# The depthwise convolution of a conformer module as a product of DFT spectra, with tokens in partitions

## The chip, the cores and the metric

The kernel runs on one core of a Trainium2 chip. The metric is the device time of one execution in microseconds (us). Three runs of the kernel before took 1069.94, 1071.75 and 1069.94 us, so its median is 1069.94 us. Of the core's engines this text names TensorE (PE, with its weight load PEld), VectorE (DVE), ScalarE (ACT), GpSimd (POOL) and SyncE (SP, which issues the DMAs).

## The reference

Two transformer blocks act on 256 tokens of width 1024. The change lies in the conv module that opens the second block:

```python
def causal_dwconv_2(x, w, b):            # w: 31 taps x 1024 channels
    y = lax.conv_general_dilated(x, w[:, None, :], window_strides=(1,),
        padding=[(30, 0)], feature_group_count=1024)
    return y + b

def conformer_conv(h, w_pw1, b_pw1, w_dw, b_dw, ln_g, ln_b, w_pw2, b_pw2):
    u = h @ w_pw1 + b_pw1                # 1024 -> 2048
    a, gate = jnp.split(u, 2, axis=-1)
    u = a * jax.nn.sigmoid(gate)
    u = causal_dwconv_2(u, w_dw, b_dw)   # each channel by itself, over time
    u = jax.nn.silu(layernorm(u, ln_g, ln_b))
    return u @ w_pw2 + b_pw2             # 1024 -> 1024
```

`h` is the RMS norm of the residual; everything is fp32. Ahead of the module stands the first block with its feed-forward part (matrix ff2 last), behind it a gated feed-forward part, an attention layer and another feed-forward part.

## The kernel before, in words

The residual `hT` lies with features in partitions: eight tiles of 128 features by 256 tokens. A value that goes through TensorE is split into two fp32r parts, high and low, and a product is three matmuls (high by high, high by low, low by high). Weights come in chunks of 128 x 1024 fp32 (512 KB), in the order of a plan: SP issues the DMA into one of 5 `raw` buffers (L327), ACT rounds it into `hi` (L335), DVE subtracts into `lo` (L336), 7 buffers each; a `raw` buffer is free again after that. `split` (L423, L424) does the same for an activation. PSUM has eight banks under three tags: 4 `acc`, 2 `up`, 2 `ms`. The order in which an engine runs its instructions is drawn up at compile time from the order of the calls, with later calls moved ahead where a cost model sees an engine idle; at run time each engine keeps that order.

The conv module takes its steps in the order of a handwritten list, `CONV_ORDER`:

- **P** (first pointwise product, w_pw1): eight pairs of a value tile and a gate tile, 48 matmuls of 256 columns each, into an `up` bank.
- **G** (`glu`, L929 to L934): scale by the norm's row, sigmoid on ACT (L389), product, into a tile `upad` with 31 leading zeros.
- The convolution itself is divided between two engines, by tap and channel tile. **D** (`conv_dve`, L948): one DVE instruction of 128x256 for each tap. **S** (`conv_rows`, L953, L957): `upad` goes out to a DRAM buffer `far` and comes back four times as `ur`, so that eight shifted copies of a channel lie in eight partitions. **E** (`conv_pe`): POOL builds a sparse weight `dw` (L966), and TensorE adds the taps up in matmuls with 32 output rows (`pcv`). **A** adds both shares (L975, L977).
- **m**, **d**, **M**: mean, deviation and squares of the layer norm over the partitions, through matmuls with a matrix of ones (`pmu`, `pmd`, `pvar`), and then normalising (L1035, L1036), SiLU (L389) and split on the eight tiles.
- The second pointwise product (`pw`, 192 matmuls of 256 columns) accumulates in the 4 `acc` banks; `residual` (L740) adds it to `hT`, and the feed-forward part follows (`ps_up`).

Between P and this product the layer norm is a barrier: it needs the convolution of all 1024 channels. The row of the norm ahead of the module (`ssa`, `ssb`) is computed in the shadow of the first P steps.

Of the kernel before, what the change touches and what calls it, by code (L numbers as in the profile page):

```python
# [28 lines left out]
CONV_ORDER = "P0 G0 P1 P2 G1 P4 P3 G2 P6 G4 D1 S1 S0 G3 S2 E2 S4 A2 P5 P7 G6 E1 G5 D0 E4 A1 A4 S3 S6 G7 E0 A0 D2 w0 E6 E3 A3 w1 S5 E5 S7 m0 d0 E7 A5 w2 D3 M0 A6 d1 A7 w3 d2 M2 M4 d3 M6 M7"  # L29
FRONT_ORDER = "D0 X2 Z0 Q0 S0 X0 W0 Z1 W1 b0 L0 u2 u4 X1 u1 Q1 u0 Q2 L1 T0 E0 B0 G0 T1 u3 Y0 W4 G1 Y1 y0 b4 W2 W5 Q3 b1 W3 b2 V0 W6 y1 n0 W7 b3 b6 V1 b5 O1 b7 O3 O0 O2 a0 s0 N0 q0 w0 q1 o0 w1 w2 o1 w3 o2 o3"  # L30
NSA_ORDER = "W1 K1 W0 R1 G0 K0 H0 g0 p0 h0 R0 H1 n0 r0 C0 p1 n1 w0 h1 V0 w1 V1 c0 t0 r1 c1 p2 C1 u0 t1 n2 w2 u1 c2 w3 o0 p3 r2 w4 t2 o1 n3 u2 t3 w5 r3 o2 w6 o3 t4 c3 w7 t5 t6 o4 o5 u3 t7 o6 o7"
PW_ORDER = (0, 1, 2, 4, 3, 6, 5, 7)
PW_PE = (8, 5, 0, 4, 7, 8, 6, 8)
# [23 lines left out]
def _plan():  # L57
# [51 lines left out]
    for j in PW_ORDER:  # L109
        both("pw1", "conv_w_pw1_2", 0, j, D)  # L110
# [34 lines left out]
def _dve_taps():  # L145

    return [(j, k) for j in range(8) for k in range(31) if (k + 1) % 8 >= PW_PE[j]]


def _rows4(w):  # L150

    w = np.concatenate([np.zeros_like(w[:1]), w], axis=0).reshape(4, 8, 8, 4, 32)
    return w.transpose(0, 4, 2, 1, 3).reshape(P, 256)
# [12 lines left out]
def _w2(w):  # L166
# [20 lines left out]
    ("b_pw1", 16, lambda I: _col(I["conv_b_pw1_2"], 16)),  # L187
    ("w_dw", 256, lambda I: _rows4(I["conv_w_dw_2"][0])),
    ("w_dv", len(_dve_taps()), lambda I: _taps(I["conv_w_dw_2"][0], 8)[:, [31 * j + k for j, k in _dve_taps()]]),
    ("b_dw", 8, lambda I: _col(I["conv_b_dw_2"], 8)),  # L190
# [18 lines left out]
def _offsets(items):  # L209
    o, out = 0, {}  # L210
    for name, n, *_ in items:
# [8 lines left out]
         ("cos", T), ("sin", T), ("cmpadd", 64), ("cmpmul", 64), ("eye4", 32), ("sbmask", P), ("cmask", P)]  # L220
# [3 lines left out]
def _constants():  # L224
# [18 lines left out]
    c["eye4"] = i % 32 == j[:, :32]  # L243
# [23 lines left out]
def kernel(ctx: ExitStack, tc: tile.TileContext, x: bass.AP, mem: bass.AP, stream: bass.AP,  # L267
# [6 lines left out]
    dpool = ctx.enter_context(tc.tile_pool(name="dpool", bufs=2, space=bass.MemoryType.DRAM))  # L274
# [166 lines left out]
    def rt(r):  # L441

        return r.row() if isinstance(r, Norm) else r
# [477 lines left out]
    yc = apool.tile([P, ND, T], F32, tag="b8", name="yc")  # L921
    NH = 31
    dve_taps = _dve_taps()

    def glu(j, ps):

        rt(rs)
        ag = spool.tile([P, 2, T], F32, tag="t2", name="ag", bufs=NT2)
        dve.tensor_mul(ag, ps, rb(rs))  # L929
        sg = spool.tile([P, T], F32, tag="t1", name="sg", bufs=NT1)  # L930
        fn(sg, ag[:, 1, :], AF.Sigmoid, bias=vec("b_pw1", 8 + j))
        up = spool.tile([P, NH + T], F32, tag="t1", name="upad", bufs=NT1)
        pool.memset(up[:, 0:NH], 0.0)
        dve.scalar_tensor_tensor(up[:, NH:], ag[:, 0, :], vec("b_pw1", j), sg, op0=ALU.add, op1=ALU.mult)  # L934
        return up

    def conv_dve(*js):

        first = {j: max([t for t in dve_taps if t[0] == j], default=None) for j in js}
        for k in range(30, -1, -1):  # L940
            for j in js:
                if (j, k) not in dve_taps:
                    continue
                w, u = vec("w_dv", dve_taps.index((j, k))), ups[j][:, k + 1:k + 1 + T]
                if (j, k) == first[j]:
                    act.activation(yc[:, j, :], u, AF.Identity, scale=w, bias=vec("b_dw", j))
                else:
                    dve.scalar_tensor_tensor(yc[:, j, :], u, w, yc[:, j, :], op0=ALU.mult, op1=ALU.add)  # L948

    def conv_rows(up):  # L950

        far = dpool.tile([P, NH + T], F32, tag="far", name="far")
        nc.sync.dma_start(far, up)  # L953
        r = apool.tile([P, 4, T + 7], F32, tag="c4", name="ur", bufs=NC4)
        for b in range(4):
            f = far[32 * b:32 * b + 32]
            nc.sync.dma_start(r[:, b, :], bass.AP(f.tensor, f.offset, [[8, 4], [NH + T, 32], [1, T + 7]]))  # L957
        return r

    def conv_pe(j):  # L960

        ps = acc_bank([P, T], "pcv")
        n = PW_PE[j]
        d = wpool.tile([P, 8, 4, 32], F32, tag="lo", name="dw", bufs=7)
        src = vec("w_dw", 32 * j, 4 * n).rearrange("p (g b) -> p g b", b=4)
        pool.tensor_mul(d[:, :n], src[:, :, :, None].to_broadcast([P, n, 4, 32]),  # L966
                        con("eye4")[:, None, None, :].to_broadcast([P, n, 4, 32]))
        for g in range(n):
            for b in range(4):
                mm(ps[32 * b:32 * b + 32, :], d[:, g, b, :], uss[j][:, b, g:g + T], g == 0, g == n - 1)  # L970
        return ps

    def conv_sum(j, ps):
        if PW_PE[j] == 8:
            act.activation(yc[:, j, :], ps, AF.Identity, bias=vec("b_dw", j))  # L975
        else:
            dve.tensor_add(yc[:, j, :], ps, yc[:, j, :])  # L977


    ups, uss, pcs, pss, w4, ln = {}, {}, {}, {}, [], {}  # L980

    def conv_mean():
        pmu = ms_bank([P, T], "pmu")
        m = spool.tile([P, T], F32, tag="t1", name="yp", bufs=NT1)
        pool.tensor_add(m, yc[:, 0, :], yc[:, 1, :])
        for i, y in enumerate((m, yc[:, 2, :], yc[:, 3, :])):
            mm(pmu, ones, y, i == 0, i == 2)
# [4 lines left out]
    def deviate(p):  # L992
        s = slice(2 * p, 2 * p + 2)
        dve.tensor_sub(yc[:, s, :], yc[:, s, :], rb(ln["mu"]))
# [450 lines left out]
```

## Time and profile before

| | us |
|---|---|
| Median of three runs | 1069.94 |
| Profiled execution, its own time | 1071.3 |
| Its span, first to last instruction | 1069.5 |
| PE / PEld busy | 1035.4 / 957.5 |
| DVE / ACT / POOL busy | 734.8 / 579.7 / 60.2 |

Times in the rows count from the start of the span. A busy PE isn't a PE at its peak: matmuls are pipelined, one of 256 columns shows as about 0.28 us and the next starts after about 0.12 us. The granted clock (PEclk) is a share of 2.4 GHz; 0.5 of it is the lower level of 1.2 GHz, and a value between is a mean over a stretch.

### The profile page before, as it was taken

Reading aid. Unit: us, or ns where it says so; the run is one execution under the profiler, and the core shown is the slowest. Engines: PE = TensorE matmul, PEld = TensorE weight load, DVE = VectorE, ACT = ScalarE, POOL = GpSimd, SP = SyncE. Lnnn points to the kernel's source line nnn. Section 1 sums busy time; section 2 is a strip of 40 time slices with the busy share of each in tenths; the row PEclk is TensorE's granted clock in tenths of the full one; section 3 lists DMA queues with packets and bytes.
Section 4 is the critical chain, followed back from the end, with each engine's and each line's share of the span. In section 5 each row is a group of like instructions: output and inputs, shape, how many; then the busy total and the mean of one; then the engine's idle time right before and its main releaser. Section 6 shows DMA issues by size and latency. Waiting matters only on the chain.

```text
span 1069.5 us, 20182 instructions
## 1 busy us (share of the span) xinstructions
PE 1035.4 (97%) x8113; PEld 957.5 (90%) x8113; DVE 734.8 (69%) x1163; ACT 579.7 (54%) x968; POOL 60.2 (6%) x148
## 2 busy tenths in 40 slices
PE   7999999999999999778999999999999999999998
PEld 6998898999999999537999999998786799999997
DVE  5976568745545587955876677766887468667673
ACT  5766657644444473215654555553867656555551
POOL 0000000000000000320000000000124300000000
PEclk9999999999999999879999999999999999999999
DMA  8753234355655655352555555644742045656641
GB/s 307 241 182 119 79 119 157 131 186 176 195 182 173 195 168 155 96 165 76 186 187 179 181 189 167 197 156 139 226 139 60 2 126 190 199 177 196 182 154 40
DMA packets 52813, 170.43 MB, mean 159 GB/s; under 512 B 5744, under 2 KB 13168, under 8 KB 52720
## 3 DMA queue, kind: packets, MB, share of 16 engines
q1 hardware_dynamic: 51952, 168.09, 48.8%
q8 instruction: 64, 1.05, 0.4%
q0 software_dynamic: 768, 1.05, 0.4%
q14 instruction: 29, 0.24, 0.1%
HBM read 165.99 MB, written 2.08 MB: 157 GB/s over the span
## 4 chain that ended last, share of the span: by engine, by line
PE 87%; DMA 6%; DVE 5%; ACT 1%; issue 1%; SPq 0%; DVEq 0%; ACTq 0%
PE ps_up L288 23%; PE ff L288 9%; PE ps_ff L288 8%; PE ob L288 6%; PE dn L288 6%; PE ps_v L288 3%; PE nl L288 2%; PE pw L288 2%; PE ps_qk L288 2%; PE no L288 2%; PE wo L288 2%; DMA far<-upad 2%; PE npo L288 2%; DVE yc L948 2%; PE ps_nq L288 2%; DMA ur<-far 2%
## 5 line engine op out<-in xcount | busy, mean ns | idle before, releaser
L336 DVE TENSOR_TENSOR lo<-raw,hi 128x1024 fp32r<-128x1024 f32 x296 | 358.2, 1223 | 169.1 <-ACT hi L335 157.3
L335 ACT ACTIVATE hi<-raw 128x1024 fp32r<-128x1024 f32 x296 | 305.2, 1049 | 261.6 <-PE ps_up L288 62.9
L288 PE MATMUL ps_up<-xh,hi 128*128 128x256 f32 x704 | 199.6, 284 | 0.3 <-DVE fv L1057 0.3
L288 PE MATMUL ps_up<-xl,hi 128*128 128x256 f32 x704 | 199.5, 283 | 0.0
L288 PE MATMUL ps_up<-xh,lo 128*128 128x256 f32 x704 | 199.2, 283 | 0.0
L288 PEld LDWEIGHTS ps_up<-xh,hi 128*128 128x128 f32 x704 | 135.1, 192 | 0.9 <-DVE fv L1057 0.5
L288 PEld LDWEIGHTS ps_up<-xl,hi 128*128 128x128 f32 x704 | 135.1, 192 | 0.4
L288 PEld LDWEIGHTS ps_up<-xh,lo 128*128 128x128 f32 x704 | 135.1, 192 | 0.0
L288 PE MATMUL ff<-us,hi 128*128 128x256 f32 x512 | 92.8, 283 | 0.0
L288 PEld LDWEIGHTS ff<-us,hi 128*128 128x128 f32 x512 | 79.4, 190 | 0.2
L288 PE MATMUL ps_ff<-xh,hi 128*128 128x256 f32 x256 | 72.7, 284 | 0.2 <-DVE fr L871 0.2
L288 PE MATMUL ps_ff<-xl,hi 128*128 128x256 f32 x256 | 72.4, 283 | 0.0
L288 PE MATMUL ps_ff<-xh,lo 128*128 128x256 f32 x256 | 72.4, 283 | 0.0
L288 PE MATMUL ff<-us,lo 128*128 128x256 f32 x256 | 72.1, 282 | 0.0
L288 PE MATMUL dn<-us,hi 128*128 128x256 f32 x352 | 63.5, 282 | 0.0
L288 PE MATMUL ob<-hi,us 128*128 128x512 f32 x176 | 56.2, 392 | 0.0
L288 PEld LDWEIGHTS dn<-us,hi 128*128 128x128 f32 x352 | 54.6, 191 | 0.0
L288 PE MATMUL dn<-us,lo 128*128 128x256 f32 x176 | 49.7, 282 | 0.0
L288 PEld LDWEIGHTS ps_ff<-xh,hi 128*128 128x128 f32 x256 | 49.1, 192 | 0.4 <-PE ps_ff L288 0.4
L288 PEld LDWEIGHTS ps_ff<-xl,hi 128*128 128x128 f32 x256 | 49.1, 192 | 0.0
L288 PEld LDWEIGHTS ps_ff<-xh,lo 128*128 128x128 f32 x256 | 49.1, 192 | 0.0
L288 PEld LDWEIGHTS ff<-us,lo 128*128 128x128 f32 x256 | 48.7, 190 | 0.0
(417 smaller groups left out, 2394.6 us busy)
## 6 DMA issues: line engine op xcount, KB each, us to landing
raw<-in_stream_dram SPq DMA_DIRECT2D x302, 512.0 KB
ur<-far SPq DMA_DIRECT2D x28, 131.5 KB
xin<-in_mem_dram SPq DMA_DIRECT2D x4, 256.0 KB
xin<-in_x_dram SPq DMA_DIRECT2D x4, 256.0 KB
out_dram<-htok SPq DMA_DIRECT2D x4, 256.0 KB
far<-upad SPq DMA_DIRECT2D x7, 143.5 KB
ct<-in_cons_dram SPq DMA_DIRECT2D x1, 720.0 KB
vt<-in_vecs_dram SPq DMA_DIRECT2D x1, 539.0 KB
```

The lines of the kernel that those rows point to most:

```text
L288: pe.matmul(ps, l, r, start=start, stop=stop, skip_group_check=True, **kw)
L335: act.activation(hi[:, :width], raw[:, :width], AF.Copy)
L336: dve.tensor_sub(lo[:, :width], raw[:, :width], hi[:, :width].bitcast(F32))
L948: dve.scalar_tensor_tensor(yc[:, j, :], u, w, yc[:, j, :], op0=ALU.mult, op1=ALU.add)
```

## The change

The convolution becomes a product of spectra. Each block of 128 output tokens takes 160 input tokens, 32 of them from the block before. A real DFT of length 160 has 79 complex frequencies and two real ones; a complex product is done with three real ones, so the spectrum has 3 x 79 + 2 = 239 rows, put into 256 (row 255 carries the bias). Three constant matrices (`fm`, `fh` for the block and for its 32 earlier tokens, `g` for the way back) and the spectrum matrix of the taps, `kw`, form one chunk of the weight stream; the taps' spectra `v` are computed on the chip by four fp32 matmuls.

From the first pointwise product to the layer norm, tokens now lie in partitions and 512 channels in columns. `project` computes one half of the gates or values: 4 chunks, 48 matmuls of 512 columns into two `acc` banks (t = 0, 1). `forward` is 6 (t = 0) or 12 (t = 1) matmuls of 512 columns, a product with `v` on DVE and a split, twice; `back` is 6 matmuls; mean and variance come from `bn_stats` along the columns. Sixteen transposes turn the result back, and ACT's SiLU applies gain and bias of the norm. The two chunks `dft` and `taps` take two of the 5 `raw` buffers until `tap_spectra` has read them, and the `hi` and `lo` of `dft` stay until the last `back`.

All of `glu`, `conv_dve`, `conv_rows`, `conv_pe`, `conv_sum`, `conv_mean`, `deviate`, `moments` goes, with their list of steps, the DRAM buffers and 351 of the 1078 columns of the vector table `vt`. The second pointwise product, and all before and behind the module, stay.

```diff
-    for j in PW_ORDER:
-        both("pw1", "conv_w_pw1_2", 0, j, D)
+    add(("dft", 0), 1024, lambda I: _dft())
+    add(("taps", 0), 256, lambda I: ...)
+    add(("b_pw1", 0), 16, lambda I: I["conv_b_pw1_2"][0].reshape(P, 16))
+    for b in range(2):
+        wide(("g", b), D + 512 * b)
+        wide(("a", b), 512 * b)
...
+    def dft_load():
+        raw, _ = raw_chunk(("dft", 0))
+        taps = wpool.tile([P, 1024], F32, tag="raw", name="taps", bufs=5)
+        nc.sync.dma_start(taps[0:32], stream[off:off + 32 * D].rearrange("(p c) -> p c", p=32))
+        act.activation(hi[:, :768], raw[:, :768], AF.Copy)
+        dve.tensor_sub(lo[:, :768], raw[:, :768], hi[:, :768].bitcast(F32))
...
+    def tap_spectra(m):
+        for b in range(2):
+            ps = (up_bank, ms_bank)[m]([P, 512], "ps_sp")
+            mm(ps, cv["raw"][0:32, 768 + P * m:768 + P * m + P], cv["taps"][0:32, s], True, True)
+            act.activation(cv["v"][:, m, s], ps, AF.Copy)
+    def project(key):
+        cv[key] = ps = [acc_bank([P, 512], "ps_pw%d" % t) for t in range(2)]
+        nc.sync.dma_start(bb, bass.AP(row.tensor, row.offset, [[0, P], [1, 512]]))
+        for k in range(4):
+            w = chunk((key, k), 512)
+            for t in range(2):
+                for kt in range(2):
+                    mm_a(ps[t], xs, 2 * k + kt, ...)
+            if key == ("g", 0) and k == 2:
+                nm.row()
+        if key == ("g", 0):
+            cv["col"] = tok_col(nm)
+    def biased(key, t):
+        dve.scalar_tensor_tensor(y, cv[key][t], cv["col"][:, t:t + 1], cv["b", key], op0=ALU.mult, op1=ALU.add)
+    def gates_of(b):
+        cv["s", b] = [biased(("g", b), t) for t in range(2)]
+        for s in cv["s", b]:
+            fn(s, s, AF.Sigmoid)
+    def glu(b):
+        for t in range(2):
+            y = biased(("a", b), t)
+            dve.tensor_mul(y, y, cv["s", b][t])
+            split(cv["u"], (slice(None), t, slice(512 * b, 512 * b + 512)), y)
+    def forward(b, t, banks):
+        for m in range(2):
+            ps = banks([P, 512], "ps_f")
+            for k in range(t + 1):
+                mm(ps, fh, u.h[:, t - k, s], k == 0, False)
+                mm(ps, fh, u.l[:, t - k, s], False, False)
+                mm(ps, fl, u.h[:, t - k, s], False, k == t)
+            dve.scalar_tensor_tensor(y, ps, con("pad")[:, m:m + 1], cv["v"][:, m, s], op0=ALU.add, op1=ALU.mult)
+            split(q, slice(None), y)
+    def back(b, t, banks):
+        for m in range(2):
+            mm(ps, gh, q.h, m == 0, False)
+            mm(ps, gh, q.l, False, False)
+            mm(ps, gl, q.h, False, m == 1)
+        dve.bn_stats(cv["st", t][:, b, :], ps)
+    def normed(t):
+        dve.bn_aggr(mv, cv["st", t])
+        fn(r[:, 0:1], mv[:, 1:2], AF.Ln, bias=eps2)
+        fn(r[:, 0:1], r[:, 0:1], AF.Exp, scale=-0.5)
+        dve.scalar_tensor_tensor(r[:, 1:2], mv[:, 0:1], -1.0, r[:, 0:1], op0=ALU.mult, op1=ALU.mult)
+        for b in range(2):
+            if b:
+                dve.tensor_scalar(y, cv["y", b, t], mv[:, 0:1], r[:, 0:1], op0=ALU.subtract, op1=ALU.mult)
+            else:
+                act.activation(y, cv["y", b, t], AF.Identity, scale=r[:, 0:1], bias=r[:, 1:2])
+    def feature(p, t):
+        if not t:
+            cv["t", p] = (up_bank if p < 2 else acc_bank)([P, 2, T], "ps_t")
+        for i in range(2):
+            pe.transpose(cv["t", p][:, i, P * t:P * t + P], ..., ident)
+    def activated(p):
+        for i in range(2):
+            fn(y[:, i, :], cv["t", p][:, i, :], AF.Silu, scale=vec("ln_g", f), bias=vec("ln_b", f))
+            split(ys, (slice(None), f), y[:, i, :])
+    project(("g", 0)); dft_load(); gates_of(0); project(("a", 0))
+    tap_spectra(0); tap_spectra(1); glu(0)
+    project(("g", 1)); gates_of(1); project(("a", 1)); glu(1)
+    w4 = [chunk(("pw2", j), D) for j in range(2)]
+    forward(0, 0, acc_bank); forward(0, 1, up_bank); forward(1, 0, acc_bank); back(0, 0, up_bank)
+    forward(1, 1, acc_bank); back(1, 0, up_bank); back(0, 1, ms_bank)
+    normed(0); back(1, 1, ms_bank)
+    w4 += [chunk(("pw2", j), D) for j in range(2, 4)]
+    for p in range(4): feature(p, 0)
+    normed(1)
+    for p in range(4): feature(p, 1); activated(p)
     acc = Acc("pw2")
+    for p in range(2):
+        acc.add(("pw2", 2 * p), ys, 2 * p, w4[2 * p:2 * p + 2])
     nm2.h()
     acc.last(("pw2", 4), ys, 4, ys, 6)
```

## Rows read from the trace of the kernel before

**Rows 1.** The page: the span, busy time by engine, the granted clock in 40 slices of the span (26.7 us each), and the chain that ended last by engine.

```profile
span 1069.5 us, 20182 instructions
PE 1035.4 (97%) x8113; PEld 957.5 (90%) x8113; DVE 734.8 (69%) x1163; ACT 579.7 (54%) x968; POOL 60.2 (6%) x148
PEclk9999999999999999879999999999999999999999
PE 87%; DMA 6%; DVE 5%; ACT 1%; issue 1%; SPq 0%; DVEq 0%; ACTq 0%
```

**Rows 2.** The chain that ended last, in order of time, from the end of ff2 to the feed-forward part behind the module: start, length, and what it was.

```profile
383.80 7.19 PE ps_pw L288 x60
...
405.46 8.15 DMA ur<-far
...
413.71 12.37 DMA far<-upad
...
457.20 7.46 DMA far<-upad
...
466.43 9.30 DMA ur<-far
...
490.25 0.82 PE pw L288 x4
...
491.10 24.15 PE pw L288 x188
515.25 8.28 PE ps_up L288 x70
```

**Rows 3.** Busy time of each engine in stretches of the module (stretch, its length, then busy time and count for PE, PEld, DVE, ACT and POOL), with granted clock, share of the DMA engines and GB/s: the first product, convolution and norm, the second product; then the first 14 us alone, the first 3 us of the second product, and 14 us of the feed-forward part behind it.

```profile
383.60:439.30 55.70, 50.30 (x396) 49.56 (x395) 47.51 (x81) 30.01 (x47) 5.83 (x8) 0.94 0.54 164
439.30:490.20 50.90, 35.94 (x391) 18.53 (x390) 36.41 (x59) 12.68 (x22) 11.20 (x13) 0.87 0.42 123
490.20:515.30 25.10, 25.02 (x194) 24.73 (x195) 14.10 (x25) 15.64 (x27) 0.06 (x1) 0.93 0.28 86
...
384.00:398.00 14.00, 13.05 (x103) 12.62 (x102) 14.00 (x21) 12.82 (x24) 0.13 (x1) 1.00 0.62 198
...
490.00:493.00 3.00, 2.72 (x13) 2.44 (x14) 2.65 (x7) 3.00 (x9) 0.10 (x1) 0.63 0.00 0
...
516.00:530.00 14.00, 13.66 (x111) 13.27 (x111) 13.47 (x20) 10.02 (x15) 0.00 (x0) 1.00 0.63 217
```

**Rows 4.** The chain again, at runs of equal matmuls: 96 of 256 columns in fp32r, 24 of 512 columns in fp32r (`ob`), one fp32 matmul of 512 columns (two records), four transposes of 128 x 128 (eight records).

```profile
545.27 11.52 PE ps_up L288 x96
...
901.32 5.47 PE ob L288 x24
...
746.76 0.86 PE rot L288 x2
...
841.27 0.87 PE npt L1301 x8
```

**Rows 5.** Groups of instructions by line with their shapes: total busy time, mean ns of one, and the idle time of the engine before them. The first two and the last four are of the stretch of the module, from 383 to 516 us (PE's up to 491 us).

```profile
L948 DVE SCALAR_TENSOR_TENSOR yc<-upad,vt,yc 128x256 f32<-128x256 f32 x66 | 31.5, 528 | 0.1
L288 PE MATMUL pcv<-ur,dw 128*32 128x256 f32 x368 | 30.6, 448 | 10.4 <-DMA ur<-far 10.4
...
L424 DVE TENSOR_TENSOR us<-fu,us 128x512 fp32r<-128x512 f32 x16 | 11.1, 692 | 0.7 <-ACT us L423 0.7
L871 DVE SCALAR_TENSOR_TENSOR fr<-ps_ff,rs 128x512 f32<-128x512 f32 x16 | 11.0, 691 | 8.9 <-PE ps_ff L288 8.9
L1255 DVE TENSOR_REDUCE nnm<-nl 128x2 f32<-128x512 f32 x16 | 10.9, 687 | 3.9 <-PE nl L288 3.9
...
L423 ACT ACTIVATE us<-fu 128x512 fp32r<-128x512 f32 x16 | 10.1, 632 | 0.5
...
L385 ACT ACT_TABLE_LOAD x4 | 5.1, 1283 | 0.1
L389 ACT ACTIVATE yc<-yc,vt 128x256 f32<-128x256 f32 x8 | 4.3, 588 | 0.0
L423 ACT ACTIVATE xh<-yc 128x256 fp32r<-128x256 f32 x8 | 2.8, 402 | 0.0
L389 ACT ACTIVATE rl<-rl 128x256 f32<-128x256 f32 x1 | 0.4, 416 | 0.0
```

**Rows 6.** DVE in order of time: start, time from the first start to the last end, and count; instructions back to back.

```profile
394.60 2.35 DVE L336 TENSOR_TENSOR lo<-raw,hi 128x1024 fp32r<-128x1024 f32 x2
...
487.61 1.29 DVE L1036 TENSOR_TENSOR yc<-yc,rl 128x512 f32<-128x512 f32 x2
```

**Rows 7.** SP and ACT in order of time: two issues of a weight chunk's DMA, and the two splits that then waited for a chunk to land (in brackets the idle time before them, and on what).

```profile
453.61 0.34 SPq L327 DMA_DIRECT2D raw<-in_stream_dram  x1
...
457.62 1.12 SPq L327 DMA_DIRECT2D raw<-in_stream_dram  x1
...
457.61 1.06 ACT L335 ACTIVATE hi<-raw 128x1024 fp32r<-128x1024 f32 x1 [6.25 <-DMA raw<-in_stream_dram]
...
465.87 1.06 ACT L335 ACTIVATE hi<-raw 128x1024 fp32r<-128x1024 f32 x1 [6.85 <-DMA raw<-in_stream_dram]
```

**Rows 8.** ACT's table load ahead of the norm's SiLU and the SiLU itself, in order of time.

```profile
487.50 1.28 ACT L385 ACT_TABLE_LOAD   x1
488.80 1.09 ACT L389 ACTIVATE yc<-yc,vt 128x256 f32<-128x256 f32 x2
```

More of the change, by code (lines that the diff above doesn't have):

```diff
@@ L142, in _taps, with _dft, spectra, forth @@
     return w.T.reshape(n, P, k).transpose(1, 0, 2).reshape(P, n * k)
[L145 to L153, printed above, removed]
+def _dft():
+    n, rows = 160, 256
+    ang = 2 * np.pi / n * np.arange(n)
+    def spectra(p, turn):
+        m = np.zeros((len(p), rows))
+        for f in range(1, 80):
+            c, s = np.cos(ang[f * p % n]), np.sin(ang[f * p % n])
+            for i, col in enumerate(turn(c, s)):
+                m[:, 3 * (f - 1) + i] = col
+        m[:, 237], m[:, 238] = 1.0, (-1.0) ** p
+        return m
+    def forth(c, s):
+        return c - s, c, -s
+    fm = spectra(32 + np.arange(P), forth)
+    fh = np.zeros((P, rows))
+    fh[96:] = spectra(np.arange(32), forth)
+    g = spectra(32 + np.arange(P), lambda c, s: (2 * (c - s), -2 * s, -2 * c)) / n
+    g[:, 255] = 1.0
+    kw = np.zeros((P, rows))
+    kw[:31] = spectra(30 - np.arange(31), lambda c, s: (c, -s - c, c - s))
+    kw[31, 255] = 1.0
+    g = g.T.reshape(2, P, P).transpose(1, 0, 2).reshape(P, 256)
+    return np.concatenate([fm, fh, g, kw], axis=1)
 def _top(v, n):
@@ L918 @@
     xs, rs = nm.xs, nm
[L921 to L987, printed above, removed]
-        ln["mu"] = spool.tile([P, T], F32, tag="t1", name="mu", bufs=NT1)
-        act.activation(ln["mu"], pmu, AF.Copy, scale=1.0 / (4 * P))
-        ln["var"], ln["md"] = up_bank([P, T], "pvar"), ms_bank([P, T], "pmd")
@@ new lines @@
+    project(("g", 0))
+    dft_load()
+    gates_of(0)
+    project(("a", 0))
+    for m in range(2):
+        tap_spectra(m)
+    glu(0)
+    project(("g", 1))
+    gates_of(1)
+    project(("a", 1))
+    glu(1)
+    w4 = [chunk(("pw2", j), D) for j in range(2)]
+    forward(0, 0, acc_bank)
+    forward(0, 1, up_bank)
+    forward(1, 0, acc_bank)
+    back(0, 0, up_bank)
+    forward(1, 1, acc_bank)
+    back(1, 0, up_bank)
+    back(0, 1, ms_bank)
+    normed(0)
+    back(1, 1, ms_bank)
+    w4 += [chunk(("pw2", j), D) for j in range(2, 4)]
```

106 lines of the change are left out of this document (50 added, 56 removed).

## The prediction

> **What bounds the kernel now.** I read the page first: TensorE is busy for 97% of the span and makes up 87% of the chain that ended last [rows 1]. So in most of the kernel only a shorter matmul stream would count. The exception stands in two places of the same rows: the granted clock has its only dip (8 and 7 tenths) in slices 17 and 18, 427 to 481 us, and the chain has 6% DMA and 5% DVE in it. Next the chain in order of time [rows 2], to see whose those shares are: between the first product (from 383.80 us) and the second (490.25 us) it runs through `far` and `ur`, the trip of `upad` through DRAM, four pieces of 7.5 to 12.4 us. Last the stretches [rows 3]. The module takes from 383.8 us (first `ps_pw`) to 515.25 us [rows 2], 131.4 us. From 439.3 to 490.2 us TensorE is busy for 35.9 of 50.9 us, largely on 368 matmuls of 32 output rows, and DVE for 36.4, largely on its 66 taps (31.5 us over the module) [rows 5]. No engine is full over the whole stretch: a chain of DMA, DVE and TensorE in turn is what the 106.4 us from 383.8 to 490.25 consist of. That is the stretch the change replaces. From 490.25 on, 192 matmuls take 25.0 us.
>
> **Rates.** In fp32r, 96 matmuls of 256 columns took 11.52 us, 0.120 each, and 24 of 512 columns 5.47 us, 0.228 each; an fp32 matmul of 512 columns took 0.86, four transposes 0.87 [rows 4]. DVE takes 0.69 us for 128x512, whether it has two or three operands and whether it reads PSUM [rows 5], and back to back one starts 0.61 after the other (1.29 for two, less 0.68); a `lo` of a chunk 1.13 to 1.23 [rows 6].
>
> **First product.** Four `project` of 48 matmuls: 192 x 0.228 = 43.8 us (before: 384 x 0.120 = 46.1 at full clock, and 55.7 in fact). Beside it stand on TensorE `ssa` and `ssb`, three fp32 matmuls of 256 columns, 3 x 0.43 = 1.3; the taps' spectra, four fp32 matmuls of 512 columns, 3.4 (32 rows instead of 128 I take to save nothing); and `tok_col`, two tiny ones, 0.4. Can the others feed it? DVE: 16 chunks and `dft` at about 1.18 = 20, two chunks of the second product 2.4, six of the eight `biased` 4.1, products and splits of the first half 2.5, the norm's sums and splits at the start some 7: 36 of 49 us, and the eight products of `nm2.h()` fit in or slip behind. DMA: 18 chunks and `dft` at 0.524 MB, `taps` 0.13 and four bias tiles of 0.26 are 11.1 MB in 49 us, 227 GB/s; 217 ran at a DMA share of 0.63 [rows 3]. So TensorE sets the pace, but not at the start: in the first 14 us DVE was busy for all 14, and TensorE lost 1 us [rows 3]; the same sums and splits stand there in the new kernel, and the column of the norm is queued on TensorE ahead of the second `project`, behind ACT's two steps on the norm's row. I take 2 us, between 1 (as now) and 5. The last matmul of `project(a, 1)` then starts to end at 383.8 + 43.8 + 1.3 + 3.4 + 0.4 + 2 = 434.7 us.
>
> The edit that holds two `raw` buffers until the spectra are taken leaves three for the chunks of `a, 0`. The trace has no such case; what bounds it is a chunk's turnaround. From issue to the split that waited it took 4.0 us once and 8.25 us once [rows 7], then 1.06 for `hi` and 1.23 for `lo`: 6.3 to 10.5 us, over three buffers 2.1 to 3.5 us a chunk, where TensorE asks for one every 12 x 0.228 = 2.74. Cost 0 to 3 us (four chunks by 0.76); I take 0, since 8.25 was beside the small rows of `ur`, which go.
>
> **From there to the second product.** TensorE: `forward` 36 x 0.228 = 8.2, `back` 24 x 0.228 = 5.5, transposes 16 x 0.217 = 3.5: 17.2 us. DVE in the same stretch: five instructions of `glu(1)` (the first `biased` runs beside the last matmuls), 16 of `forward` (product and split, eight times), four `bn_stats`, one normalisation of t = 0: 26 of 128x512 at 0.61 = 15.9, and two chunks of the second product 2.4: 18.3 us. ACT has ten splits and a normalisation, and is not the bound. So DVE is last here, with TensorE beside it. Behind its last `bn_stats` a short chain is bare: aggregate 0.16, Ln and Exp at most 0.42 each, the shift 0.16, the normalisation 0.69, some hops: 2 us; a table load of 1.28 [rows 8]; SiLU 0.59 and `hi` 0.40 [rows 5]; hops 0.3. The transposes fit beside the load. 18.3 + 2.0 + 1.3 + 1.3 = 22.9 us, so the second product starts at 457.6 instead of 490.25: 32.7 us earlier.
>
> `bn_stats` has no row. Nearest is the reduction of 128x512 from PSUM at 0.69 [rows 5]; from below half of that, from above two passes, 1.4: -1.3 to +2.8 us for four. I take one pass. The two later chunks of `w4` may be split in this stretch too: 0 to +2.3.
>
> ACT's load of a table took 1.28 us and the SiLU started 0.02 us behind it [rows 8]. The Trainium skill (ScalarE: Activation LUTs, What ACT_TABLE_LOAD costs) gives as much for the load but adds a drain of about 1.4 us to every switch. By the row the two switches here (Ln and Exp, SiLU) cost what the sum has; by the page they would cost 2.8 us more. The row decides.
>
> **Second product and after.** It keeps its 192 matmuls. Before, 25.0 us rather than 192 x 0.120 = 23.0 because the clock stood at 0.63 of full in its first 3 us [rows 3], behind the norm's bare chain. TensorE again has only transposes in the last microseconds ahead of it, and two of the four `acc` banks are free only when ACT has read the third and fourth transposed pair, 5 to 6.6 us after the first SiLU's start at ACT's 1.66 us a pair, about when the first `add` reaches them. I keep 25.0 us, bounds 23 and 27. Behind the module nothing changes: `residual` and the next norm are the same, and the feed-forward part starts as late behind the second product as now. The smaller `vt` saves bytes that nobody waits for: TensorE runs there.
>
> **Sum.** The profiled execution took 1071.3 us (span 1069.5). 1071.3 - 32.7 = 1038.6; the median of runs shown is 1.4 us below the profiled execution, so 1037 us.
>
> **Rivals.**
> *Everything overlaps.* If the model's order puts `forward` of the first half into the gaps of the last `project`, only TensorE counts: 383.8 + 43.8 + 1.3 + 3.4 + 0.4 + 1 + 17.2 + 3 of SiLU path = 453.9, and the product at 23 us: 38.4 us gained, 1031. This is the lower end of the forecast, not a case by itself. Its upper end takes the unlucky ends of the unknown costs together: 3 + 3 + 2.8 + 2.3 + 2 = 13, 1050.
>
> *The stages of the transform don't overlap.* Engines keep their compiled order, and `up` and `ms` have two banks each, so a `back` may wait for a product that stands behind another one on DVE. One after the other: `forward` 3.7 us (1.37 of matmuls, product 0.69, `hi` 0.63 and `lo` 0.69 behind them [rows 5], hops) or 5.1, twice each, `back` 2.1 four times, `glu(1)` 4, norm, transposes and SiLU 7: 37 us instead of 23, and 4 more lost in the first product. 18 us later, 1055. For it: at 405 to 439 us the chain of now shows just such waits [rows 2]. Against: the two halves and two token blocks are independent of each other.
>
> *The clock stays low.* In the stretch from 439.3 us the granted clock was 0.87 on the mean with TensorE busy for 71% of it [rows 3]. Here it would be busy for some 75% of 23 us. At 1.2 GHz the 13.7 us of `forward` and `back` become 27.4; with the transposes (3.5, twice that at worst) TensorE passes DVE and takes 34 instead of 23: 1048.
>
> *The weights starve, and the kernel is slower.* Place: the `raw` queue, in all four `project`s, if spectra are taken late (their matmuls placed behind more chunks) and SP, which issues in order, stands before a bias tile whose buffer isn't free. Price: 16 chunks by the turnaround over three buffers, less 2.74. It eats the 33 us from 4.8 us a chunk on, a landing of 12 us; at 14 us, 16 x (5.4 - 2.74) = 43 us, 1080. For it: 8.25 us have been seen [rows 7]. Against: that was under 131 KB row shuffles that are gone, and DMA has room by the bytes.
>
> *The convolution was covered anyway.* Then nothing would be gained: 1070. Against it stands the chain, which goes through `far` and `ur` [rows 2], and TensorE's 15 idle us.
>
> **Chances.** Forecast with its ends (1031 to 1050) 0.65; stages in series 0.17; low clock 0.10; starving weights 0.05; covered anyway 0.03. The range of 8 in 10 reaches from 1029 to 1056. A measurement of this kernel tells apart about 0.2%, 2 us. Faster by more: 0.65 + 0.17 + 0.10 = 0.92; same 0.02; slower 0.06 (0.05, and a third of the last case).
>
> **What would show it.** Right: `far`, `ur`, `dw` and POOL's work gone; four blocks of 48 matmuls at 0.228 us; the last one done at 433 to 437 us; the second product's first matmul at 455 to 460 us with DVE over 80% busy in the 20 us before it; granted clock above 0.9 there. Wrong in the first product: gaps on TensorE that end with `lo` or a landing of `raw`. Wrong in the transform: TensorE waiting for DVE or ACT in every `back`, or DVE idle. The whole would be wrong if DVE had slack in the old stretch that another wait took, or `bn_stats` on PSUM cost several passes.

## The result and the profile after

The kernel with the change takes 1038.94 us (median of four runs, 1036.84 to 1040.04), the kernel before 1069.94 us on the same chip: a ratio of 0.9709, 95% interval 0.9696 to 0.9722. The forecast was 1037 us within 1029 to 1056. The profiled execution of after took 1040.04 us, its span is 1037.8.

The page of after: span, busy time by engine, granted clock in 40 slices, the chain by engine, and the DMA of the weight chunks (last column: median us from issue to landing). It answers to [rows 1].

```profile
span 1037.8 us, 19034 instructions
...
PE 1018.8 (98%) x7619; PEld 943.3 (91%) x7619; DVE 707.4 (68%) x1107; ACT 583.1 (56%) x970; POOL 43.6 (4%) x128
...
PEclk9999999999999999989999999999999999999999
...
PE 92%; DVE 4%; DMA 2%; ACT 1%; issue 1%; SPq 0%; POOL 0%; DVEq 0%; ACTq 0%; POOLq 0%
...
raw<-in_stream_dram SPq DMA_DIRECT2D x303, 512.0 KB, 4.1
```

TensorE is busy 16.6 us less, the span is 31.7 us shorter: about half of what went is TensorE's waiting. Where it went is read from the chain of after in order of time (start, length, what), which answers to [rows 2]:

```profile
383.01 8.19 PE ps_pw L309 x36
...
397.41 9.52 PE ps_pw L309 x41
406.94 4.00 PE ps_sp L309 x8
410.94 22.10 PE ps_pw L309 x84
...
435.35 1.41 DVE pw L987 x2
...
445.52 0.61 DVE bst L1031
...
452.91 1.14 DVE lo L357
454.04 0.72 DVE yn L1044
454.76 0.13 DVE bmv L1036
454.92 0.30 ACT brs L410
455.24 0.20 ACT brs L410
455.46 1.28 ACT L406
456.76 0.79 ACT yn L1046
457.55 0.04 issue
457.59 0.70 PE ps_t L1055 x2
458.32 1.02 ACT ya L410 x2
459.34 0.31 ACT xh L444
459.69 23.99 PE pw L309 x192
483.69 8.28 PE ps_up L309 x69
```

`far` and `ur` are gone, and with them every DMA in this part of the chain. It now runs on TensorE to 433 us, through the `hi` and `lo` of a weight chunk on ACT and DVE, on DVE alone from 435.35 to 454.76, and then changes engine at every step up to the second product. The feed-forward part follows at 483.69 instead of 515.25 [rows 2], 31.56 us earlier; the span is 31.7 us shorter, so behind the module nothing was won or lost. Of the 31.56 us, 29.8 lie between the first `ps_pw` and the first `pw` (76.8 instead of 106.6 us), 1.0 in the second product (24.0 instead of 25.0), and 0.8 ahead of the first `ps_pw`, where nothing was edited; in the profiles below that point lies between 382.53 and 384.51. The first `ps_pw` is dated here by the start of its matmul, in before and in after:

```profile
383.64 0.28 PE L288 MATMUL ps_pw<-xh,hi 128*128 128x256 f32 x1
...
382.85 0.40 PE L309 MATMUL ps_pw<-hi,xh 128*128 128x512 f32 x1
```

The chain dates the same matmul 0.16 us later (383.80 and 383.01); the 106.4 us of the prediction count from there.

Stretches of after, in the columns of [rows 3]: 13 us around the taps' spectra, and within them two short ones; then the transform with the norm, its last 4.7 us, and the first 3 us and the whole of the second product.

```profile
407.00:420.00 13.00, 13.00 (x36) 8.55 (x37) 6.02 (x8) 5.69 (x9) 0.00 (x0) 0.74 0.66 217
411.00:413.00 2.00, 2.00 (x5) 1.61 (x6) 0.79 (x2) 1.09 (x2) 0.00 (x0) 0.50 1.00 182
...
417.00:419.00 2.00, 2.00 (x10) 1.65 (x9) 1.23 (x1) 0.45 (x1) 0.00 (x0) 1.00 0.01 2
435.60:459.70 24.10, 18.45 (x78) 13.74 (x76) 20.19 (x35) 13.52 (x23) 0.00 (x0) 0.89 0.22 66
455.00:459.70 4.70, 3.33 (x15) 2.53 (x14) 0.91 (x3) 3.86 (x8) 0.00 (x0) 0.50 0.42 120
459.70:462.70 3.00, 3.00 (x19) 3.00 (x20) 1.50 (x4) 3.00 (x9) 0.00 (x0) 0.74 0.00 0
459.70:483.70 24.00, 24.00 (x194) 24.00 (x195) 13.10 (x23) 15.31 (x27) 0.00 (x0) 0.97 0.28 90
```

Two things stand in it. In the transform DVE is busy for 20.19 of 24.1 us, TensorE for 18.45: DVE is the fuller engine, and the idle part of it is the last five microseconds. And the granted clock stood at its lower level (0.50) behind the spectra, with TensorE busy for every microsecond from 407 to 420. TensorE in order of time shows that fall in the matmuls themselves:

```profile
406.87 4.08 PE L309 MATMUL ps_sp<-taps,raw 32*128 32x512 f32 x8
...
412.32 0.63 PE L309 MATMUL ps_pw<-hi,xh 128*128 128x512 f32 x1
412.75 0.63 PE L309 MATMUL ps_pw<-lo,xh 128*128 128x512 f32 x1
```

One `ps_pw` starts 0.43 us after the other, where 0.228 is the rule [rows 4]. The 13 us at 0.74 of full have cost 13 x 0.26 = 3.4 us.

### The profile page after: what moved, and what is told of

Same layout as the page of the kernel before. It is cut to its first block, busy times and chain, and to the rows that moved or that the text cites. A ratio compares the mean times of both kernels' runs of the same rounds, so it can differ in the third digit from the quotient of the medians.

```text
span 1037.8 us, 19034 instructions
## 1 busy us (share of the span) xinstructions
PE 1018.8 (98%) x7619; PEld 943.3 (91%) x7619; DVE 707.4 (68%) x1107; ACT 583.1 (56%) x970; POOL 43.6 (4%) x128
## 3 DMA queue, kind: packets, MB, share of 16 engines
q1 hardware_dynamic: 48016, 164.80, 49.1%
## 4 chain that ended last, share of the span: by engine, by line
PE 92%; DVE 4%; DMA 2%; ACT 1%; issue 1%; SPq 0%; POOL 0%; DVEq 0%; ACTq 0%; POOLq 0%
PE ps_up L309 24%; PE ff L309 9%; PE ps_ff L309 9%; PE dn L309 6%; PE ob L309 6%; PE ps_pw L309 4%; PE ps_v L309 3%; PE nl L309 2%; PE pw L309 2%; PE ps_qk L309 2%; PE no L309 2%; PE wo L309 2%; PE npo L309 2%; PE ps_nq L309 2%; PE ps_xbc L309 2%; DVE lo L357 1%
## 5 line engine op out<-in xcount | busy, mean ns | idle before, releaser
L309 PE MATMUL ps_ff<-xl,hi 128*128 128x256 f32 x256 | 72.4, 283 | 0.0
L309 PE MATMUL ps_ff<-xh,lo 128*128 128x256 f32 x256 | 72.4, 283 | 0.0
L309 PEld LDWEIGHTS ps_ff<-xh,hi 128*128 128x128 f32 x256 | 49.1, 192 | 0.4 <-PE ps_ff L309 0.4
L309 PEld LDWEIGHTS ps_ff<-xl,hi 128*128 128x128 f32 x256 | 49.1, 192 | 0.0
L309 PEld LDWEIGHTS ff<-us,lo 128*128 128x128 f32 x256 | 49.1, 192 | 0.0
L309 PEld LDWEIGHTS ps_ff<-xh,lo 128*128 128x128 f32 x256 | 49.1, 192 | 0.0
```

The lines of the kernel that those rows point to most:

```text
L309: pe.matmul(ps, l, r, start=start, stop=stop, skip_group_check=True, **kw)
```

## The experiments

The theory: the exposed convolution is what went; in the first product TensorE sets the pace and loses time only by the fall of its clock; in the transform DVE is last, and behind it a bare chain. The rivals: the layout, not the convolution, made the gain; TensorE or a wait of one engine for another is last in the transform; the first product lacks weights, or the spectra themselves are what is dear.

Three lengths are compared throughout: the *first product*, from the first `ps_pw` to the first `ps_f`; the *transform* with the norm, from there to the first `pw`; and the *stretch*, the two together. All in us, from the one profiled execution of each kernel; "clock" is the granted clock from 407 to 420 us, "whole" the time of the kernel (a single run, or a median with the number of runs). The chips differ: beside e1 to e4 the kernel before took 1066.21 us in a single run, beside e5 to e8 1069.26, and beside e9 to e12 1069.61 (median of nine). So the last column compares well only within e9 to e12.

| kernel | first product | transform | stretch | clock | whole |
|---|---|---|---|---|---|
| before | | | 106.6 | | 1069.94 (4) |
| after | 52.7 | 24.1 | 76.8 | 0.74 | 1038.94 (4) |
| e1_rows128 | 49.1 | 24.1 | 73.2 | 1.00 | 1038.26 |
| e2_spread | 50.8 | 24.1 | 75.0 | 1.00 | 1040.54 |
| e3_late | 50.1 | 24.1 | 74.2 | 1.00 | 1038.65 |
| e4_q_hi | 52.8 | 19.7 | 72.4 | 0.74 | 1036.11 |
| e5_before_no_conv | | | 66.2 | 1.00 | 1030.19 |
| e6_after_no_conv | | | 56.1 | 1.00 | 1022.38 |
| e7_tail | 49.5 | 22.5 | 72.1 | 1.00 | 1035.5 |
| e8_all | 48.8 | 21.7 | 70.5 | | 1034.32 |
| e9_after_again | 51.2 | 24.1 | 75.3 | 0.87 | 1039.85 (5) |
| e10_rows128_again | 49.2 | 24.1 | 73.3 | 1.00 | 1038.50 (4) |
| e11_all2 | 48.7 | 19.4 | 68.1 | | 1033.39 (4) |
| e12_no_late | 49.2 | 21.3 | 70.5 | 1.00 | 1034.79 (4) |

### What the convolution costs in either kernel

In before, 30 of its 31 taps are left out, so that none is left on DVE or TensorE; ACT applies the last one:

```diff
-PW_PE = (8, 5, 0, 4, 7, 8, 6, 8)
+PW_PE = (0, 0, 0, 0, 0, 0, 0, 0)
...
-    return [(j, k) for j in range(8) for k in range(31) if (k + 1) % 8 >= PW_PE[j]]
+    return [(j, 30) for j in range(8)]
```

> The kernel before with 30 of the 31 taps of the convolution left out (ACT applies the last one; no DVE taps, no trip through DRAM, no matmuls with 32 output rows). From the first matmul of the first product to the first of the second it took 106.4 us with the convolution. My theory, that the convolution and the waits it brings are what the stretch was long by: 46 us of first product, 2 to 4 of sums and stalls, some 9 of the layer norm over partitions: 58 to 62 us. Rival, the layout is what costs (norm over partitions, 256-column matmuls, waits for the up banks): 75 us or more stay without the convolution.

In after, the transform, the spectra and `dft` are left out, and the statistics are taken of the gated product:

```diff
-            dve.tensor_mul(y, y, cv["s", b][t])
-            split(cv["u"], (slice(None), t, slice(512 * b, 512 * b + 512)), y)
+            dve.tensor_mul(cv["u"][:, t, 512 * b:512 * b + 512], y, cv["s", b][t])
+            cv["y", b, t] = cv["u"][:, t, 512 * b:512 * b + 512]
...
+            dve.bn_stats(cv["st", t][:, b, :], cv["y", b, t])
...
-    dft_load()
...
-    for m in range(2):
-        tap_spectra(m)
...
-    forward(0, 0, acc_bank)
...
-    back(1, 1, ms_bank)
```

> The changed kernel with the transform left out: the layer norm reads the gated product itself; no spectra, no forward, no back. The same stretch took 76.8 us with the transform. My theory: 43.7 + 1.3 + 0.5 of matmuls, then gating, statistics, normalisation, transposes and SiLU, about 10: 54 to 58 us, so the layout by itself is worth some 2 to 6 us against the kernel before without its convolution, and the price of the convolution fell from about 46 to about 20. Rival, the layout is worth most of the gain: 45 us or less, or 20 us less than the kernel before without its convolution.

The stretch came to 66.2 and 56.1 us. So the convolution's exposed price was 106.6 - 66.2 = 40.4 us, and it is 76.8 - 56.1 = 20.7 now: 19.7 us won. The other 66.2 - 56.1 = 10.1 us come from the layout: more than the 2 to 6 expected, and 66.2 lies between the two theories, nearer to the lower. TensorE of e5 in order of time shows why (in brackets the idle time before, and on what):

```profile
437.83 1.22 PE L288 MATMUL pvar<-sq,ct 128*128 128x256 f32 x2 [4.90 <-POOL sq L1001]
...
449.05 1.22 PE L288 MATMUL pw<-xh,hi 128*128 128x256 f32 x4 [4.59 <-ACT xh L423]
```

The last `ps_pw` ends at 431.64, and the old norm, with its sums over the partitions by matmuls, takes 17.4 us from there to the second product. In e6 it is 10.2 us, from the same point at 428.69 to 438.90; the remaining 2.9 us of the 10.1 are the first product (48.8 us of `ps_pw` in e5, 45.9 in e6).

### Is DVE last in the transform?

The low part of `q` is left out, and the matmul that reads it:

```diff
-            split(q, slice(None), y)
+            act.activation(q.h, y, AF.Copy)
...
-            mm(ps, gh, q.l, False, False)
```

> Leaves out the low part of the products of spectra: eight splits on DVE of 128x512 and eight of the 24 matmuls of back go, so the convolution is less exact. Transform (first matmul of forward to the first of the second product) 24.1 us in the changed kernel. Theory A, DVE is last there: 8 x 0.61 = 4.9 us shorter, 19.2. Theory B, TensorE is last: 8 x 0.228 = 1.8 us shorter, 22.3. Theory C, it is a chain of single latencies (the stages don't overlap): the low part's 0.69 us four to eight times plus matmuls, 4 to 7 us shorter, with DVE idle in between.

The transform fell by 4.4 us to 19.7. Eight subtractions of 0.61 are 4.9 on DVE; eight matmuls of 0.228 are 1.8 on TensorE. The loss is DVE's. In its stretch DVE is busy for 15.59 us, about 4.6 less than in after, and TensorE for 2.5 less:

```profile
435.30:455.00 19.70, 15.97 (x70) 12.64 (x68) 15.59 (x27) 13.45 (x23) 0.00 (x0) 0.88 0.25 81
...
435.44 5.89 PE ps_f L309 x26
```

The second line is the chain of e4 at the start of the transform. It stays on TensorE to 447.09 us: with less for DVE to do TensorE is last, so the 4.9 could not come whole. Theory C does not fit: DVE waits for 0.3 us in all before its last aggregate.

### What stands in the first product?

Three kernels change the taps' spectra alone. e1_rows128 lets them run over all 128 rows, the upper 96 filled with zeros:

```diff
+        pool.memset(taps, 0.0)
...
-            mm(ps, cv["raw"][0:32, 768 + P * m:768 + P * m + P], cv["taps"][0:32, s], True, True)
+            mm(ps, cv["raw"][:, 768 + P * m:768 + P * m + P], cv["taps"][:, s], True, True)
```

> The four fp32 matmuls for the taps' spectra take 128 rows instead of 32 (the 96 added ones hold zeros in both operands; the result is the same). In the changed kernel they take 4.1 us, and behind them the granted clock is at its lower level for some 6 us, which costs about 3 us: first product 52.6 us from its first matmul to the first of forward. Theory A, the 32 used rows lowered the clock: clock 1.0 behind the spectra, first product about 49.6 us, whole time 3 us shorter. Theory B, it is four fp32 matmuls in a row whatever their rows, or the zeros count as little as absent rows: unchanged, 52.6 us.

e2_spread takes them one at a time, 24 other matmuls apart:

```diff
...
-    project(("a", 0))
-    for m in range(2):
-        tap_spectra(m)
+    project(("a", 0), lambda k: k % 2 and tap_spectra(k // 2, (0,)))
...
-    project(("g", 1))
+    project(("g", 1), lambda k: k % 2 and tap_spectra(k // 2, (1,)))
```

> The same four fp32 matmuls of 32 rows, but one at a time, 24 full matmuls apart, in the second and third project. If only their standing together (4.1 us without a full matmul) lowers the clock: clock 1.0 throughout, first product about 49.6 us instead of 52.6, whole time about 1036. If each costs its share wherever it stands: 52.6 us. The four matmuls themselves keep 0.86 to 1 us each.

e3_late takes them behind the last `project`, so that two `raw` buffers are held through all four of them:

```diff
     project(("a", 0))
-    for m in range(2):
-        tap_spectra(m)
     glu(0)
     project(("g", 1))
     gates_of(1)
     project(("a", 1))
+    for m in range(2):
+        tap_spectra(m)
     glu(1)
```

> The spectra are computed behind the last project instead of the second, so the two raw buffers are held through all of the first product. My theory (three buffers are enough: landing 4.1 us, two splits 2.3 us, 2.1 us a chunk where TensorE asks for one every 2.74): first product some 7 us shorter by the spectra and their clock dip, transform longer by 4 to 8 us, whole time within 3 us of the changed kernel, no gaps on TensorE that end with raw. The rival of the prediction (weights starve): eight more chunks at 3.5 us or more, TensorE waiting for hi or lo in the third and fourth project, 6 us or more lost there.

With 128 rows the clock stayed at 1.00, and the first product took 49.1 us instead of 52.7. Its single run shows nothing of this in the whole: 1038.26 us is 0.974 of before on its chip, where after stands at 0.971. The spectra themselves took 3.6 us, and 3.7 on 32 rows where the clock did not fall (e7_tail below), so their price is not in the rows:

```profile
407.00:420.00 13.00, 13.00 (x52) 9.44 (x51) 7.52 (x10) 7.56 (x10) 0.00 (x0) 1.00 0.86 257
```

Spread, the clock stayed up too, but each lone fp32 matmul cost more: from the `ps_pw` ahead of the first one to the `ps_pw` behind it 1.37 us passed, 1.14 more than a `ps_pw` alone, where 3.6 / 4 = 0.9 is the price in a block. The gain from the clock was half eaten, and the whole, expected at about 1036 us, was 1040.54 in a single run.

Late, `ps_pw` took 45.8 us from the first to the end without a gap on TensorE. Two buffers held through the whole of it cost nothing: the rival that weights starve is refuted. The clock fell there as well, behind the spectra, now in the transform; in stretches of 2 us from 432 us it reads 0.63, 0.50, 0.50, 0.67 with TensorE busy throughout, and the transform's mean is 0.78:

```profile
433.90:457.90 24.00, 20.21 (x77) 16.22 (x76) 16.49 (x28) 11.47 (x21) 0.00 (x0) 0.78 0.25 87
```

The transform is as long as in after, 24.1 us, though DVE has 3.7 us less to do in it (16.49 busy instead of 20.19): its work on the last values now runs beside the spectra. The chain of e3 is on TensorE there, and its first 24 `ps_f` take 2.8 us longer at the lower clock than those of e11_all2 below (e3, then e11):

```profile
433.95 8.23 PE ps_f L309 x24
...
433.78 5.45 PE ps_f L309 x24
```

So what the late place won, the fall of the clock took back. The transposes of e3 also wait 3.69 us behind a table load, as told of e7 below. e12_no_late and e11_all2 below, with 128 rows and no such fall, differ in this edit alone: 21.3 and 19.4 us.

Two kernels run several times on one chip ask how much of this is left in the whole: after unaltered, and e1's kernel again.

> The changed kernel again, unaltered, to stand beside the next three on one chip. Behind its 32-row spectra the clock fell to its lower level in the executions of this kernel and of two kernels alike there, and not in the one with both moves of the tail, where the spectra stand 0.3 us elsewhere in time. If the fall depends on where the 4 us lie, these executions differ among themselves by about 3 us with the mean clock (0.993 with the fall, 0.997 without); if it always comes, they all show 0.993 or 0.994. Median 1036 to 1040 us.

> Spectra with 128 rows. If 32 used rows lower the clock and 128 don't: mean clock 0.996 or more in every execution, median about 3 us below the changed kernel on the same chip (0.3%). If the earlier look was luck: some executions with 0.993, and the median within 1 us of the changed kernel.

The medians are 1039.85 (1038.91 to 1041.63) and 1038.50 us (1037.82 to 1038.54): 1.35 us apart, where 3 were expected. Every execution of e10 is below every one of e9, but the ratios' intervals (0.9707 to 0.9742, and 0.9694 to 0.9725), which hold the scatter of before too, overlap. The profiles say why it is less. After's second profile has a shorter fall:

```profile
407.00:420.00 13.00, 13.00 (x43) 8.85 (x42) 7.03 (x9) 6.30 (x9) 0.00 (x0) 0.87 0.76 236
```

That is 13 x 0.13 = 1.7 us, half of the 3.4 in the first, and near the 1.35. By the sign of the expectation the fall always comes in after: its nine executions have a mean clock of 0.993 or 0.994, and the four of e10 have 0.995. The mean does not tell how long each fall was, since the clock at the end of the module varies as well: from 450 to 490 us it is 0.91 in after and e7, and 0.87 in e9 and e10. e7_tail below has the same four matmuls with 32 rows and no fall, though they start where those of e4 do, which has it (406.57 and 406.54 us). With the block of four on 32 rows it came in four profiles (after, e9, e3 and e4) and not in one (e7); on 128 rows it came in none of five. What decides when it comes was not found.

### The bare end of the transform

The chain of after has things in its last seven microseconds that need not stand there: a `lo` of `w4` (1.14 us) and a normalisation of t = 0 (0.72) ahead of the last aggregate, and the table load ahead of ACT's normalisation of t = 1. e7_tail puts the splits of the two later `w4` chunks behind the last normalisation, and both normalisations of t = 1 on DVE:

```diff
...
+        if behind is not None:
+            after(i, behind)
...
-            if b:
+            if b or t:
...
-    w4 += [chunk(("pw2", j), D) for j in range(2, 4)]
...
     normed(1)
+    w4 += [chunk(("pw2", j), D, cv["last"]) for j in range(2, 4)]
```

> Two moves behind the last statistics of the norm, nothing left out: the low parts of two chunks of the second product are put behind the last normalisation on DVE (they stood between its last statistics), and for t = 1 both halves are normalised on DVE, since ACT's half stood behind a table load of 1.28 us. Transform 24.1 us in the changed kernel. If DVE's queue is what is last there, and ACT's load behind it: 2.3 + 1.2 = 3.5 us shorter, 20 to 21 us. If TensorE or a single chain of latencies is last elsewhere: less than 1 us.

The transform took 22.5 us: 1.6 us less than after, which is less than expected. ACT of e7 in order of time shows the wait that took the place:

```profile
448.70 1.28 ACT L408 ACT_TABLE_LOAD   x1
450.00 0.78 ACT L1048 ACTIVATE yn<-ps_y,brs 128x512 f32<-128x512 f32 x1
```

The load for SiLU stands ahead of the normalisation that it does not serve, and all 16 transposes now stand behind that normalisation. TensorE of the same kernel:

```profile
450.83 3.67 PE L1057 MATMUL ps_t<-ct,yn 128*128 128x128 f32 x16 [3.69 <-ACT yn L1048]
```

It waited 3.69 us, and then ran 16 transposes in a row at the lower clock (0.50 from 450.8 to 454.6), where after had done half of them earlier. The order of an engine is drawn up at compile time; the edit moved three instructions and changed it for others too.

e8_all has e1's, e3's and e7's edits together.

> Spectra with 128 rows, computed behind the last project, and both moves of the tail; the result is the changed kernel's. First product without spectra 45.8 us; the spectra 3.6 us beside DVE's gating of the second half; the clock stays at its upper level, so the transform is DVE's again, less the gating it now does beside the spectra (3 us) and the 3.5 of the tail: 17 to 19 us. Together 67 to 69 us from the first matmul of the first product to the first of the second, 8 to 10 us less than the changed kernel's 76.8. If the holding of the raw buffers or the order of the engines takes it back: 72 us or more.

The stretch came to 70.5 us: with the same order on ACT and the same wait of 3.69 us on the normalisation, it missed by 1.5 what was expected. e11_all2 is e8_all with one more edit: the normalisation on ACT goes through `fn`, the helper that keeps a table load behind all users of the table before it, so the load for SiLU cannot pass it. e12_no_late is e11_all2 without the late spectra.

```diff
-                act.activation(y, cv["y", b, t], AF.Identity, scale=r[:, 0:1], bias=r[:, 1:2])
+                fn(y, cv["y", b, t], AF.Identity, scale=r[:, 0:1], bias=r[:, 1:2])
```

> All four edits (spectra with 128 rows, behind the last project; lows of two chunks behind the normalisation; t = 1 normalised on DVE), and ACT's Identity for t = 0 tied to the table that is loaded, so that the load for SiLU can't go ahead of it: in the earlier kernel with all edits the transposes waited 3.7 us for that Identity, which stood behind the 1.28 us load. From the first matmul of the first product to the first of the second 69 us, against 70.5 there and 76.8 in the changed kernel; whole time 7 to 8 us below the changed kernel on this chip (0.7 to 0.8%).

> As the kernel with all edits, but the spectra stay behind the second project. It tells what their place is worth once the clock is out of the way: behind the last project they cover the gating of the second half (3 us of DVE while TensorE works on them), so here the whole should be 1 to 3 us longer than with all edits; the same within 0.5 us if TensorE has enough of forward to do there anyway.

With the load tied, the wait of the transposes fell from 3.69 to 2.46 us, and the stretch to 68.1 us, 0.9 less than expected; ACT of e11:

```profile
449.02 0.78 ACT L412 ACTIVATE yn<-ps_y,brs 128x512 f32<-128x512 f32 x1
449.81 1.28 ACT L408 ACT_TABLE_LOAD   x1
```

The whole is 1033.39 us (median of four, 1030.99 to 1035.35; ratio to before 0.9662, 0.9641 to 0.9684), against 1039.85 for after on the same chip: 6.5 us less, where 7 to 8 were expected, and the fastest kernel of this study. Its four executions are two pairs: 1035.12 and 1035.35 us with a mean clock of 0.996 and 0.997, and 1031.65 and 1030.99 with 0.999 and 1.000. The median lies between them, and the profile is of the first. The stretch is 7.2 us shorter than in e9_after_again. Its chain is on TensorE from 428.99 to 447.18 us: with the spectra late DVE no longer comes last. Some of it was given back at the next place, which stretches of e11 show (the first 3 us of the second product, and the whole of it):

```profile
452.60:455.60 3.00, 2.45 (x9) 2.16 (x10) 3.00 (x6) 3.00 (x9) 0.00 (x0) 0.50 0.69 198
452.60:478.70 26.10, 25.55 (x194) 25.26 (x195) 17.12 (x27) 15.31 (x27) 0.00 (x0) 0.90 0.57 183
```

The second product takes 26.1 us there instead of 24.0 in after: TensorE waits in it for a low part of the SiLU's output, for which DVE is late because it first does the two moved splits (the chain of e11 has 2.27 us of `lo` just ahead of it), and the clock starts low. e12_no_late is 1.4 us above e11 (1034.79, 1034.1 to 1035.43), within what was expected, but the ranges overlap, and at the mean clock of e12's four executions (0.996 and 0.997) e11 was not faster: whether the late spectra are worth anything in the whole stays open.

## Why the prediction was right, and where two errors cancelled

The predicted sum of the profiled execution was 1038.6 us, and it took 1040.04. Step by step:

**First product.** Predicted 50.9 us up to the last `project`, measured 52.7. This is nearer than it deserves. The stall of 2 us was 0: in the first 14 us TensorE never waited, where it lost 1 us before [rows 3].

```profile
383.00:397.00 14.00, 14.00 (x64) 11.19 (x62) 12.84 (x19) 11.73 (x23) 0.10 (x1) 1.00 0.56 176
```

Spectra and `tok_col` cost 3.6 and 0.5 without a fall of the clock, 0.3 more than taken. What was not foreseen is the fall behind the spectra, 3.4 us in this profile. Without it the sum would be 43.8 + 1.3 + 3.6 + 0.5 = 49.2, and e10 and e12 have just that. The rival of the low clock was weighed in the transform alone; it came in the first product, where TensorE has no idle time, and it cost 3.4 us where the rival put 11.

**Raw buffers.** Taken at 0, bounds 0 and 3. No matmul of `project` waited, and e3 held the two buffers over all four blocks without a wait. Over the whole of after a chunk lands in 4.1 us at the median, about the shorter of the two landings in [rows 7]; that the row shuffles made the longer one is not shown.

**Transform.** Predicted 22.9 us, measured 24.1, from two terms. DVE's work up to its last normalisation of t = 0 was 18.3, and is 435.59 to 454.76, 19.2 us. Eight products at 0.66 from start to start instead of 0.61 are 0.4 of the 0.9, a sixth instruction of `glu(1)` about 0.4 (the first `biased` did not run beside the last matmuls: a `lo` of `w4` stood ahead of it on DVE until 435.35), the norm's aggregates and shift 0.2. The groups of DVE from 383 to 484 us (total busy, mean ns of one | idle before them) show the rates: what reads PSUM with a scalar per partition takes 0.74 and 0.80, not 0.69.

```profile
L1016 DVE SCALAR_TENSOR_TENSOR sy<-ps_f,ct,spec 128x512 f32<-128x512 f32 x8 | 5.6, 739 | 0.0
L445 DVE TENSOR_TENSOR sq<-sy,sq 128x512 fp32r<-128x512 f32 x8 | 5.1, 676 | 0.0
...
L1031 DVE BATCH_NORM_STATS2 bst<-ps_y 128x6 f32<-128x512 f32 x4 | 2.7, 684 | 0.0
...
L1044 DVE TENSOR_SCALAR yn<-ps_y,bmv,brs 128x512 f32<-128x512 f32 x2 | 1.6, 802 | 0.0
```

The idle time in the last column is 0.0 in each of these rows: DVE does come last, as the step said, and e4 bears it out. `bn_stats` takes 0.684 us, as long as a subtraction of the same size: one pass, the value taken between a half and two. The bare chain behind was 2.0 + 1.3 + 1.3 = 4.6, and is 459.69 - 454.76 = 4.9 us. Its size was nearly right and its order wrong: "the transposes fit beside the load" failed, since the load stood ahead of the normalisation, so 0.70 us of transposes are bare; and the first `pw` had to wait for two SiLUs in turn (1.02) instead of one (0.59). In exchange the steps up to the normalisation took 1.4 us (0.13, 0.30, 0.20 and 0.79) instead of 2.0. Two splits of chunks lie in the 19.2 us, as counted, but it is the other pair: the early one was split beside the first product, and the later one, which was given bounds of 0 to +2.3 and taken at 0, is the one in the transform.

**Table load.** ACT started the normalisation 0.02 us behind the load:

```profile
455.46 1.28 ACT L406 ACT_TABLE_LOAD   x1
456.76 0.78 ACT L1046 ACTIVATE yn<-ps_y,brs 128x512 f32<-128x512 f32 x1
```

The row was the right choice. The drain that the Trainium skill (ScalarE: Activation LUTs, What ACT_TABLE_LOAD costs) adds to a switch shows neither here nor in e7.

**Second product.** Taken 25.0, bounds 23 and 27; measured 24.0 here, 25.2 in e9, 26.1 in e11. It opens at a lower clock in each (0.74, 0.50 and 0.50 in the first 3 us), as in before (0.63) [rows 3].

**The sum.** First product +1.8, transform +1.2, second product -1.0, the start 0.95 earlier than the 383.8 taken (0.16 of it is the chain's dating): 483.69 instead of 482.6 us for the end of the module, and the rest of the span as before. The last two are luck: they are no larger than what the profiles above differ by among themselves in these places.

**The rivals.** *Everything overlaps* did not come: the transform takes 24.1 us where its matmuls alone are 17.2. *The stages don't overlap* did not either: DVE had no idle time between 435.35 and 454.76. *The weights starve* is refuted by e3. *Covered anyway* is refuted by e5 and e6: both kernels get faster without the convolution, before by 40.4 us in its stretch. Of these 40.4 the change won 19.7. The other 10.1 us came from tokens in partitions; of that the prediction priced the matmuls of the first product (43.8 for 46.1 us), and never the old norm's share by itself.

**What would show it.** Last `project` done at 433 to 437 us: 435.6. First `pw` at 455 to 460 us: 459.69. DVE over 80% busy in the 20 us before it: 16.09, which is just that.

```profile
439.70:459.70 20.00, 14.35 (x60) 10.35 (x58) 16.09 (x29) 10.58 (x19) 0.00 (x0) 0.87 0.18 52
```

Granted clock above 0.9 there: this sign failed, with 0.87 (0.89 over the transform), for the lower level in the last 5 us. In the transform it cost little, since of TensorE's work there only 0.70 us of transposes are bare.

## What to carry to other kernels

Replacing a chain that changes engine at every step by work that one engine can stream wins idle time of all of them (here 19.7 of the convolution's 40.4 us); price the chain by leaving it out of either kernel, and price a change of layout by itself, since here it was a third of the gain. Where the sum meets the measurement, look at its terms all the same: a stall that did not come and a fall of the clock that was not foreseen hid each other here. And when one engine's tail is bare, see that nothing that serves only the next stage (a split, a table load) is ordered into it, and then look at what the moved work delays there.

## What the runs showed of the hardware that was not expected

- The granted clock fell to its lower level with TensorE busy throughout, behind a block of four fp32 matmuls that use 32 rows of the array: 0.50 from 411 to 413 us in after, and 1.00 again from 417 us on. It fell in four of five profiles with such a block (all but e7), and in none of five where the same block used 128 rows. The Trainium skill (TensorE: Matmul & The Clock Gate, HAM oscillation — how this bites in real kernels) puts such falls down to idle gaps of TensorE; here there was none, and the measurement decides.
- An fp32 matmul of 512 columns took no less time on 32 rows than on 128 (3.7 us for four in e7, 3.6 in e1), as the prediction had taken it. Alone among fp32r matmuls it cost 1.14 us instead of 0.9.
- Statistics of 128x512 from PSUM (`bn_stats`) cost one pass of DVE, 0.684 us against 0.676 for a subtraction of that size, and joining two halves 0.19 us.
